# Wide projections of an attention layer: token blocks zero and one by Strassen's seven half products

## The chip, the cores and the metric

One core of a Trainium2 chip runs the whole kernel. The metric is the device time of one execution in microseconds (us). The engines are named as in the profile: PE is TensorE, DVE is VectorE, ACT is ScalarE, POOL is GpSimd, SP is SyncE; PEld is TensorE's weight load.

## The reference

One layer of a diffusion backbone: 2048 latent tokens, 256 context tokens, width 1024. One wide input projection feeds two token mixers (latent attention with a rotary key, neighbourhood attention on a 32 x 64 grid); both results are gated, projected and merged.

```python
h = rmsnorm(x, norm_g[i]) * (1 + scale) + shift
hc = rmsnorm(ctx, norm_g[i]) * (1 + scale_c) + shift_c
ckv, kr, kb, vb, cq, za, qb, zb, ga, gb = split_cols(h @ w_in[i], KV_SPLITS + Q_SPLITS)
...
oa = block_attention(qa, jnp.concatenate([ka, kca], axis=1),
                     jnp.concatenate([va, vca], axis=1), mla_scale)
ob = neighborhood_attention(heads(qb, NA_HEADS), heads(kb, NA_HEADS), heads(vb, NA_HEADS),
                            heads(c_kb, NA_HEADS), heads(c_vb, NA_HEADS), rpb[i])
ya = (oa * jax.nn.silu(za)) @ w_oa[i]
yb = (ob * jax.nn.silu(zb)) @ w_ob[i]
y = (jax.nn.sigmoid(ga) * ya + jax.nn.sigmoid(gb) * yb) @ w_out[i]
x = x + gate * y
return rmsnorm(x, final_g)
```

The change concerns `h @ w_in`: of its columns, kb, qb, za, zb (512 each) and ga, gb (1024 each) are the wide ones.

## The kernel before

**Number format.** A float32 operand is split into a high part, rounded to the matmul's reduced type by an ACT copy, and a low part, the difference, by a DVE subtraction (`split_weight`, L112 to L117). A product is then three matmuls: high by high, high by low, low by high (`mm3`, L135, which records all of them).

**Layout.** The normalised tokens lie transposed in SBUF as four blocks of 512, each with a high and a low tile of 8 x (128 x 512) (`hh`, `hl`, in pools `hT0` to `hT3`). The wide columns come in 32 chunks of 128: 0 to 3 are k, 4 to 7 q, 8 to 11 za, 12 to 15 zb, 16 to 23 ga, 24 to 31 gb. Chunks 16 and 17 are computed earlier as fillers.

**The projection stage.** One chunk is loaded (`load_chunk`, L312: `rawc`, 128 x 1024, then `whi` by ACT and `wlo` by DVE) while the one before is multiplied. `chunk` (L363 and the lines behind) runs over the token blocks in `srcs`: 24 matmuls of 128 x 512 into a PSUM bank `accm`, then an evacuation: `evac_k` (L326), `evac_q` (L341) or `evac_g` (L353 to L359, a sigmoid on ACT, for za and zb a product on DVE, and a store of 256 KB). k chunks have three blocks, since block zero is done earlier, the others four: 4 x 3 + 26 x 4 = 116 blocks.

**Raw weights.** Every raw weight of this stage goes through `raw_tile` (L306 to L309), which alternates between two pools with one raw buffer each, whatever the weight is. A load therefore waits until the weight that was loaded two calls before has been split.

**Side work.** Three generators are pumped from this loop.
- `lowrank_gen` (L599 and the lines behind): the low-rank q, k and v of the latent attention, with its stores to DRAM (`qm`, `kmS`). One step per block, for chunks below `NSIDE` = 20.
- `gate_gen` (L573): eight loads `rawg` of 512 KB with four small matmuls each. One per item from item 12.
- `presplit_gen` (L587): 16 weights of the output stage are loaded (`rawps`, 512 KB), split in two halves `ps` into the two buffers `st`, and stored (`woS`, `wfS`, L595, 512 KB each). Two per item behind item 22.

The v columns are two items of their own, `vb_load` and `vb_run` (L693, L705): each 16 tiles of 24 matmuls of 128 x 256 into `vacc`, with 256 columns of weights in pool `vw`. They stand behind items 20 and 22. The last two chunks, 30 and 31, are interleaved block by block.

**Order.** The tile framework turns the program into one order of instructions per engine and inserts the waits; most DMA loads and stores of this stage are issued by SP in program order, so an issue that waits for a buffer holds up the ones behind it. Behind the stage, SP loads `NKm` and `NQs` (L848, L849), the neighbourhood attention's keys and queries, from the stores of the k and q chunks.

The loop that sets the order:

```python
for i, (_, run_) in enumerate(items):
    cur = nxt
    if i + 1 < len(items):
        nxt = items[i + 1][0]()
    run_(cur)
    if i >= 12:
        next(gate_it, None)
    if i > NSIDE + 2:
        pump(pre_it, 2)
```

## Time and profile before

| | us |
|---|---|
| median of 3 runs | 2521.4 |
| fastest and slowest run | 2518.43, 7962.48 |
| the profiled execution, its time | 2524.23 |
| its span in the profile | 2522.5 |
| normalisation, context and fillers, about | 0 to 243 |
| projection stage | 243 to 1052 |
| attention | 1053 to 2140 |
| output stage | 2140 to 2522 |

The span runs from the first to the last instruction of the profiled execution. Busy time of an engine is the time in which it executes; a matmul's listed duration overlaps that of its neighbours, so the pace of many matmuls is read from a window or from a piece of the chain, not from one duration. The granted clock (PEclk) is given as a share of full speed.

### The profile page before, as it was taken

Reading aid. Unit: us, or ns where it says so; the run is one execution under the profiler, and the core shown is the slowest. Engines: PE = TensorE matmul, PEld = TensorE weight load, DVE = VectorE, ACT = ScalarE, POOL = GpSimd, SP = SyncE. Lnnn points to the kernel's source line nnn. Section 1 sums busy time; section 2 is a strip of 40 time slices with the busy share of each in tenths; the row PEclk is TensorE's granted clock in tenths of the full one; section 3 lists DMA queues with packets and bytes.
Section 4 is the critical chain, followed back from the end, with each engine's and each line's share of the span. In section 5 each row is a group of like instructions: output and inputs, shape, how many; then the busy total and the mean of one; then the engine's idle time right before and its main releaser. Section 6 shows DMA issues by size and latency. Waiting matters only on the chain.

```text
span 2522.5 us, 34848 instructions
## 1 busy us (share of the span) xinstructions
PE 2476.6 (98%) x12796; PEld 1841.1 (73%) x12796; DVE 1108.0 (44%) x2285; ACT 900.8 (36%) x1774; POOL 1092.7 (43%) x861
## 2 busy tenths in 40 slices
...
GB/s 270 194 92 167 260 222 193 126 163 192 194 164 92 115 214 204 179 94 43 105 33 130 39 111 39 124 36 111 39 130 36 59 173 93 256 184 164 179 146 72
DMA packets 182980, 342.86 MB, mean 136 GB/s; under 512 B 25130, under 2 KB 95950, under 8 KB 175438
## 3 DMA queue, kind: packets, MB, share of 16 engines
...
q10 hardware_dynamic: 432, 0.28, 0.0%
HBM read 214.42 MB, written 126.13 MB: 135 GB/s over the span
## 4 chain that ended last, share of the span: by engine, by line
PE 91%; DVE 3%; DMA 2%; ACT 2%; issue 1%; POOL 1%; SPq 0%; POOLq 0%; ACTq 0%; DVEq 0%
PE accm L135 26%; PE S L807 16%; PE oacc L807 10%; PE pm L807 5%; PE ya L135 5%; PE f L135 4%; PE vacc L135 4%; PE nacc L226 3%; PE no L807 3%; PE accf L135 2%; PE accx L135 1%; PE nm L807 1%; PE pstl L185 1%; PE qa_False L135 1%; ACT P L1278 1%
## 5 line engine op out<-in xcount | busy, mean ns | idle before, releaser
L1288 POOL TENSOR_TENSOR za<-za,P 128x1024 f32<-128x1024 f32 x217 | 516.4, 2380 | 97.0 <-ACT P L1278 90.3
L825 DVE TENSOR_REDUCE m<-pm 128x1 f32<-128x512 f32 (+1 forms) x640 | 385.9, 632 | 284.4 <-PE pm L807 278.0
L1278 ACT ACTIVATE P<-S 128x512 f32<-128x512 f32 x576 | 342.1, 596 | 427.9 <-PE S L807 401.3
L135 PE MATMUL accm<-hh,whi 128*128 128x512 f32 x928 | 366.7, 395 | 0.0
L135 PE MATMUL accm<-hh,wlo 128*128 128x512 f32 x928 | 366.4, 395 | 0.0
L135 PE MATMUL accm<-hl,whi 128*128 128x512 f32 x928 | 366.4, 395 | 0.0
L807 PE MATMUL oacc<-P,V 128*64 128x512 f32 x1152 | 274.9, 613 | 0.0
L807 PE MATMUL S<-qh,Kh 97*128 97x512 f32 x576 | 242.0, 420 | 9.2 <-ACT P L1278 5.1
L807 PE MATMUL S<-ql,Kh 96*128 96x512 f32 x576 | 230.4, 400 | 0.0
L807 PE MATMUL S<-qh,Kl 96*128 96x512 f32 x576 | 229.3, 398 | 0.0
L807 PE MATMUL pm<-Kh,qh 96*128 96x512 f32 (+1 forms) x640 | 214.5, 382 | 8.7 <-DVE m L825 5.8
L135 PEld LDWEIGHTS accm<-hh,whi 128*128 128x128 f32 x928 | 174.1, 188 | 42.9 <-issue 0.8
L135 PEld LDWEIGHTS accm<-hh,wlo 128*128 128x128 f32 x928 | 174.1, 188 | 42.5
L135 PEld LDWEIGHTS accm<-hl,whi 128*128 128x128 f32 x928 | 174.1, 188 | 41.5
L135 PE MATMUL ya<-u,woh 128*128 128x256 f32 x1024 | 184.9, 283 | 0.7 <-DVE t L1346 0.7
L807 PEld LDWEIGHTS oacc<-P,V 128*64 128x64 f32 x1152 | 75.7, 139 | 150.1 <-issue 150.1
L807 PEld LDWEIGHTS pm<-Kh,qh 96*128 96x128 f32 x640 | 120.2, 188 | 73.0 <-issue 29.6
L135 PE MATMUL f<-wfh,y 128*128 128x512 f32 (+1 forms) x528 | 162.2, 387 | 1.9 <-ACT y L1349 1.8
L135 PEld LDWEIGHTS ya<-u,woh 128*128 128x128 f32 x1024 | 160.1, 192 | 1.7 <-DVE t L1346 0.9
L807 PEld LDWEIGHTS S<-qh,Kh 97*128 97x128 f32 x576 | 109.5, 190 | 56.8 <-ACT P L1278 22.6
L135 PE MATMUL ya<-u,wol 128*128 128x256 f32 x512 | 144.8, 283 | 0.0
L356 ACT ACTIVATE g<-accm 128x512 f32<-128x512 f32 x88 | 52.2, 593 | 250.4 <-PE accm L135 208.1
...
## 6 DMA issues: line engine op xcount, KB each, us to landing
rawc<-in_wch SPq DMA_DIRECT2D x30, 512.0 KB
...
qR<-q SPq DMA_DIRECT2D x16, 512.0 KB
...
woS<-ps SPq DMA_DIRECT2D x16, 512.0 KB
```

The costliest lines, as they stand in the source:

```text
L135: nc.tensor.matmul(acc, a, b, start=(i == 0), stop=(i == n - 1))
L185: nc.tensor.matmul(pst[32 * j:32 * j + 32, :w], ones[:, 0:32], sq[:, :w], start=(kt < 4), stop=(kt >= 4))
L226: nc.tensor.matmul(acc[:, :n], a[:, k, sl], b[:, k, :n], start=(k == 0 and q == 0), stop=(k == KT - 1 and q == 2))
L356: nc.scalar.activation(s1, acc, AF.Sigmoid)
L807: ins = nc.tensor.matmul(*args, **kw)
L825: nc.vector.reduce_max(m5[:, qt, ci:ci + 1], pm[:, :b - a], axis=AX.X)
L1278: nc.scalar.activation(pt[:, x, :], sp, AF.Exp)
L1288: ve.tensor_tensor(za, za, pt, op=ALU.add)
```

## The change

The 26 wide chunks 4 to 15 and 18 to 31 are paired: 13 pairs of 256 columns. In a pair, token blocks zero and one against the two chunks are computed as one 2 x 2 product of halves by Strassen's scheme (in Winograd's form): the inner dimension of 1024 is halved, the two token blocks are the two columns of the token operand, and the two chunks the two columns of the weight. Seven products of 12 matmuls (L844 after) replace the 8 x 12 of four plain blocks.

- Blocks two and three of all 30 chunks are computed first, as before (`srcs = lat[2:]`), with two side steps per block. The gate and the two presplits run behind items 18 and later, chunks 20 and up.
- The v items come last: half one for tiles 8 to 15, then half zero for tiles 8 to 15 and 0 to 7. Half one for tiles 0 to 7 is loaded again at the end.
- `token_sums` builds the sums of the token halves (`t1` to `t5`), splits them and writes them into new tiles `ta`, `tb` in the pools of blocks two and three. Per k: 11 DVE, 3 POOL and 4 ACT operations of 128 x 512, for four k.
- `fast_columns` runs the pairs. Per pair it loads two raw chunks, forms the four weight sums on POOL (`s1` to `s4`), splits seven operands of 128 x 512 on ACT and DVE (`w1` to `w7`), runs the seven products into three banks `A`, `B`, `C`, of which four are accumulated on top of an earlier one, forms the sums `c1`, `u2`, `u4` on ACT and DVE, and evacuates four results.
- Then come the four k chunks of block one, and half one of v for tiles 0 to 7. The stages behind are as before.

```diff
-        srcs = lat[1:] if ci < 4 else lat
+        srcs = lat[2:]
...
+    def vb_load(hf, pl=None):
+        if pl is None and hf == 1:
             pump(side_gen, 999)
-            env["vw"] = pool(xes, "vw")
-        vw = env["vw"]
-        vhi = vw.tile([P, KT, 256], F32R, tag="vhi", name=f"vhi{hf}")
-        vlo = vw.tile([P, KT, 256], F32R, tag="vlo", name=f"vlo{hf}")
-        load_big(vw, I["wvb"][:, :, hf * 256:(hf + 1) * 256], 256, vhi, vlo, f"w{hf}")
+            env["vw"] = pool(ves, "vw")
+        vw = pl or env["vw"]
...
+    def vb_run(hf, wt, tis):
+        for ti in tis:
             vb_tile(ti, hh[ti // 4], hl[ti // 4], ti % 4, wt[0], wt[1], 2 * hf, 2)
...
-        items += [chunk_item(base + j, j, ev, 1 if base + j < NSIDE else 0) for j in range(n) if base + j not in (FILL, FILL + 1)]
-    items.insert(NSIDE, (lambda: vb_load(0), lambda wt: vb_run(0, wt)))
-    items.insert(NSIDE + 2, (lambda: vb_load(1), lambda wt: vb_run(1, wt)))
-    ev = evac_g(gbS, False)
-
-    def last_two(wt):
-        ws = (wt, load_chunk(31))
-        for sr in lat:
-            for q in range(2):
-                chunk(f"m{30 + q}", 6 + q, ws[q], [sr], ev)
-
-    items[-2:] = [(lambda: load_chunk(30), last_two)]
...
+    gate_it, pre_it = gate_gen(), presplit_gen()
...
-        if i >= 12:
+        if i >= 18:
             next(gate_it, None)
-        if i > NSIDE + 2:
             pump(pre_it, 2)
-    xes.close()
...
+    def token_sums(ph, hp, hq, pl):
+        ta, tb_ = h_tiles(2, f"ta{ph}"), h_tiles(3, f"tb{ph}")
+        def split(src, dst, k, add=None):
+            nc.scalar.activation(dst[0][:, k, :], src, AF.Copy)
+            nc.vector.tensor_tensor(dst[1][:, k, :], src, bc(dst[0][:, k, :]), op=ALU.subtract)
+        def gen():
+            for k in range(HK):
+                p1_, p2_ = [[bc(t[:, k + x * HK, :]) for t in hp] for x in range(2)]
+                q1_, q2_ = [[bc(t[:, k + x * HK, :]) for t in hq] for x in range(2)]
+                t1 = pl.tile([P, W], F32, tag="t1", name=f"t1{ph}_{k}")
+                t2 = pl.tile([P, W], F32, tag="t2", name=f"t2{ph}_{k}")
+                nc.gpsimd.tensor_tensor(t1, q1_[0], p1_[0], op=ALU.subtract)
+                nc.vector.tensor_tensor(t2, q1_[1], p1_[1], op=ALU.subtract)
+                nc.vector.tensor_tensor(t1, t1, t2, op=ALU.add)
+                split(t1, ta, k)
+                nc.vector.tensor_tensor(t2, q2_[0], t1, op=ALU.subtract)
+                nc.vector.tensor_tensor(t2, t2, q2_[1], op=ALU.add)
+                split(t2, ta, k + HK)
+                yield
+                t3 = pl.tile([P, W], F32, tag="t1", name=f"t3{ph}_{k}")
+                nc.gpsimd.tensor_tensor(t3, p2_[0], t2, op=ALU.subtract)
+                nc.vector.tensor_tensor(t3, t3, p2_[1], op=ALU.add)
+                split(t3, tb_, k + HK)
+                yield
+                t4 = pl.tile([P, W], F32, tag="t2", name=f"t4{ph}_{k}")
+                t5 = pl.tile([P, W], F32, tag="t1", name=f"t5{ph}_{k}")
+                nc.gpsimd.tensor_tensor(t4, q2_[0], q1_[0], op=ALU.subtract)
+                nc.vector.tensor_tensor(t5, q2_[1], q1_[1], op=ALU.subtract)
+                nc.vector.tensor_tensor(t4, t4, t5, op=ALU.add)
+                split(t4, tb_, k)
+                yield
+        (b11, b21), (_, b22) = halves(*hp), halves(*hq)
+        (o1, o2), (o3, o4) = halves(*ta), halves(*tb_)
+        return gen(), [b11, o2, o3, o1, b21, o4, b22]
+    pairs = []
+    for base, n, dst, silu in ((4, 4, None, 1), (8, 4, zaS, True), (12, 4, zbS, True),
+                               (16, 8, gaS, False), (24, 8, gbS, False)):
+        ev = evac_g(dst, silu) if dst is not None else evac_q
+        js = [j for j in range(n) if base + j not in (FILL, FILL + 1)]
+        pairs += [(base, js[i], js[i + 1], ev) for i in range(0, len(js), 2)]
+    def load_pair(ph, i):
+        base, a, b, _ = pairs[i]
+        return [raw_tile(I["wch"][base + j].rearrange("p k m -> p (k m)"), f"s{ph}_{base + j}").rearrange("p (x f) -> p x f", x=2)
+                for j in (a, b)]
+    def fast_columns(ph, p, q, bops, raws):
+        with ExitStack() as es:
+            wop = pool(es, "wop", 3)
+            wt_ = pool(es, "wt")
+            ct = pool(es, "ct")
+            slots = [0]
+            def slot(nm):
+                i = slots[0] % 7
+                slots[0] += 1
+                if i < 4:
+                    return env["cw"][i // 2].tile([P, KT, P], F32R, tag=("whi", "wlo")[i % 2], name=nm)
+                return wop.tile([P, KT, P], F32R, tag="op", name=nm)
+            def operand(src, nm):
+                t = slot(nm)
+                f = t.rearrange("p k m -> p (k m)")
+                nc.scalar.activation(f[:, :W], src, AF.Copy)
+                nc.vector.tensor_tensor(f[:, W:], src, bc(f[:, :W]), op=ALU.subtract)
+                return [(t[:, k, :], t[:, HK + k, :]) for k in range(HK)]
+            def tmp(tag, nm):
+                return wt_.tile([P, W], F32, tag=tag, name=nm)
+            def prep(i, ra, rb):
+                nm = f"{ph}_{i}"
+                a11, a12, a21, a22 = ra[:, 0], ra[:, 1], rb[:, 0], rb[:, 1]
+                yield operand(a11, f"w1{nm}")
+                s1, s2 = tmp("s1", f"s1{nm}"), tmp("s2", f"s2{nm}")
+                nc.gpsimd.tensor_tensor(s1, a21, a22, op=ALU.add)
+                nc.gpsimd.tensor_tensor(s2, s1, a11, op=ALU.subtract)
+                yield operand(s2, f"w6{nm}")
+                s3 = tmp("s3", f"s3{nm}")
+                nc.gpsimd.tensor_tensor(s3, a11, a21, op=ALU.subtract)
+                yield operand(s3, f"w7{nm}")
+                yield operand(s1, f"w5{nm}")
+                yield operand(a12, f"w2{nm}")
+                yield operand(a22, f"w4{nm}")
+                s4 = tmp("s3", f"s4{nm}")
+                nc.gpsimd.tensor_tensor(s4, a12, s2, op=ALU.subtract)
+                yield operand(s4, f"w3{nm}")
+            def product(acc, w_, x_, first):
+                n = 0
+                for (ah, al), (bh, bl) in zip(w_, x_):
+                    for a, b in ((ah, bh), (ah, bl), (al, bh)):
+                        nc.tensor.matmul(acc, a, b, start=(first and n == 0), stop=(n == 3 * HK - 1), skip_group_check=True)
+                        n += 1
+            def bank(nm):
+                return psA.tile([P, 512], F32, tag="acc", name=nm)
+            g = prep(0, *raws)
+            ops = list(g)
+            for i, (base, ja, jb, ev) in enumerate(pairs):
+                nm = f"{ph}_{i}"
+                nops = []
+                g = iter(())
+                if i + 1 < len(pairs):
+                    g = prep(i + 1, *load_pair(ph, i + 1))
+                def run(m, acc, first):
+                    product(acc, ops[m], bops[m], first)
+                    o = next(g, None)
+                    if o is not None:
+                        nops.append(o)
+                A = bank(f"A{nm}")
+                run(0, A, True)
+                c1 = ct.tile([P, W], F32, tag="c1", name=f"c1{nm}", bufs=2)
+                nc.scalar.activation(c1, A, AF.Copy)
+                B = bank(f"B{nm}")
+                run(1, B, True)
+                u2 = ct.tile([P, W], F32, tag="u2", name=f"u2{nm}")
+                nc.vector.tensor_tensor(u2, B, c1, op=ALU.add)
+                C_ = bank(f"C{nm}")
+                run(2, C_, True)
+                run(3, B, False)
+                u4 = ct.tile([P, W], F32, tag="u4", name=f"u4{nm}")
+                nc.vector.tensor_tensor(u4, B, c1, op=ALU.add)
+                nc.vector.tensor_tensor(u4, C_, u4, op=ALU.add)
+                ev(jb, q, u4, W)
+                run(4, A, False)
+                ev(ja, p, A, W)
+                run(5, C_, False)
+                nc.vector.tensor_tensor(u2, C_, u2, op=ALU.add)
+                ev(jb, p, u2, W)
+                run(6, B, False)
+                nc.vector.tensor_tensor(c1, B, c1, op=ALU.add)
+                ev(ja, q, c1, W)
+                ops = nops
+    tg, bops = token_sums(0, (hh[0], hl[0]), (hh[1], hl[1]), tl)
+    raws = load_pair(0, 0)
+    pump(tg, 99)
+    ves.close()
+    fast_columns(0, 0, 1, bops, raws)
+    hes2.close()
+    with ExitStack() as es:
+        vw2 = pool(es, "vw2", side="right")
+        wt2 = vb_load(1, vw2)
+        nxt = load_chunk(0)
+        for j in range(4):
+            cur = nxt
+            if j < 3:
+                nxt = load_chunk(j + 1)
+            chunk(f"n{j}", j, cur, lat[1:2], evac_k)
+        vb_run(1, wt2, range(8))
+    tes.close()
     hes.close()
     p1.close()
```

How the instructions stand now. First ACT, before, around `whi27`, the split of chunk 27: `g1_2` and `g1_3` are the evacuations of the last two blocks of chunk 25, `ps` the halves of the presplit weights.

```order
L116 ACTIVATE ps6_0_7606<-rawps6_7604 128x512
L116 ACTIVATE ps6_1_7610<-rawps6_7604 128x512
L356 ACTIVATE g1_2_7435<-accm25_2_7410 128x512
L116 ACTIVATE whi27_7488<-rawc27_7486 128x1024
L356 ACTIVATE g1_3_7463<-accm25_3_7438 128x512
L116 ACTIVATE ps7_0_7616<-rawps7_7614 128x512
L356 ACTIVATE g2_0_7517<-accm26_0_7492 128x512
L116 ACTIVATE ps7_1_7620<-rawps7_7614 128x512
L356 ACTIVATE g2_1_7545<-accm26_1_7520 128x512
```

In the changed kernel the same place on ACT reads:

```order
L356 ACTIVATE g2_3_5326<-accm26_3_5301 128x512
L116 ACTIVATE whi27_5269<-rawc27_5267 128x1024
L356 ACTIVATE g3_2_5386<-accm27_2_5361 128x512
L116 ACTIVATE ps12_0_5337<-rawps12_5335 128x512
L116 ACTIVATE ps12_1_5341<-rawps12_5335 128x512
L356 ACTIVATE g3_3_5414<-accm27_3_5389 128x512
L116 ACTIVATE ps13_0_5347<-rawps13_5345 128x512
L116 ACTIVATE ps13_1_5351<-rawps13_5345 128x512
L116 ACTIVATE whi28_5357<-rawc28_5355 128x1024
L116 ACTIVATE ps14_0_5425<-rawps14_5423 128x512
```

Before, `whi27` stood in the middle of chunk 25's evacuations, two chunks ahead of its use. Now it stands behind the last evacuation of chunk 26 (`g2_3`), and `whi28` behind that of chunk 27 (`g3_3`) and all four `ps` of its item. SP, in the changed kernel, from the gate load of item 24 on:

```order
L309 DMA rawg6_5329<-in_wmod 128x1024
L309 DMA rawps12_5335<-in_wout 128x1024
L309 DMA rawps13_5345<-in_wout 128x1024
L359 DMA gbS3_151<-g3_2_5386 128x512
L598 DMA wfS_158<-ps12_0_5337 128x2x512
L598 DMA wfS_158<-ps12_1_5341 128x2x512
L309 DMA rawc28_5355<-in_wch 128x1024
L359 DMA gbS3_151<-g3_3_5414 128x512
L598 DMA wfS_158<-ps13_0_5347 128x2x512
L598 DMA wfS_158<-ps13_1_5351 128x2x512
L309 DMA rawg7_5417<-in_wmod 128x1024
L309 DMA rawps14_5423<-in_wout 128x1024
```

The load `rawc28` stands behind the two stores of `ps12`, which is loaded in the same item, and behind the first store of chunk 27 (`g3_2`); before, it stood between two stores of chunk 25. DVE, in the changed kernel, from the place where block two's tiles come free, at the start of the products:

```order
L753 TENSOR_TENSOR hlta0_6424<-t10_0_6431,hhta0_6423 128x512
L753 TENSOR_TENSOR hlta0_6424<-t20_0_6432,hhta0_6423 128x512
L771 TENSOR_TENSOR t30_0_6442<-t30_0_6442,hl0_193 128x512
L753 TENSOR_TENSOR hltb0_6426<-t30_0_6442,hhtb0_6425 128x512
L777 TENSOR_TENSOR t50_0_6448<-hl1_787 128x512
L778 TENSOR_TENSOR t40_0_6447<-t40_0_6447,t50_0_6448 128x512
L753 TENSOR_TENSOR hltb0_6426<-t40_0_6447,hhtb0_6425 128x512
L762 TENSOR_TENSOR t20_1_6455<-hl1_787,hl0_193 128x512
L763 TENSOR_TENSOR t10_1_6454<-t10_1_6454,t20_1_6455 128x512
L765 TENSOR_TENSOR t20_1_6455<-hh1_786,t10_1_6454 128x512
L753 TENSOR_TENSOR hlta0_6424<-t10_1_6454,hhta0_6423 128x512
```

Here `hlta0` and `hltb0` are the low parts of `ta` and `tb`; these rows are one k and the start of the next, and none of them stands in the kernel before.

## Rows read from the trace of the kernel before

**Rows 1.** The page, engines' busy time and the chain that ended last by engine.

```profile
PE 2476.6 (98%) x12796; PEld 1841.1 (73%) x12796; DVE 1108.0 (44%) x2285; ACT 900.8 (36%) x1774; POOL 1092.7 (43%) x861
...
PE 91%; DVE 3%; DMA 2%; ACT 2%; issue 1%; POOL 1%; SPq 0%; POOLq 0%; ACTq 0%; DVEq 0%
```

**Rows 2.** Chain in order of time, projections: start us, us, what.

```profile
503.26 11.20 PE accm L135 x48
...
732.73 45.43 PE vacc L135 x384
```

**Rows 3.** Windows: us, busy (x) of PE, PEld, DVE, ACT, POOL; PEclk, DMA share, GB/s.

```profile
243.00:505.00 262.00, 262.00 (x1131) 210.98 (x1131) 56.30 (x76) 79.93 (x134) 40.39 (x60) 1.00 0.63 202
...
690.00:870.00 180.00, 180.00 (x1164) 161.25 (x1163) 27.76 (x42) 34.85 (x70) 14.56 (x26) 1.00 0.41 127
```

**Rows 4.** The page, DMA issues.

```profile
rawc<-in_wch SPq DMA_DIRECT2D x30, 512.0 KB
...
woS<-ps SPq DMA_DIRECT2D x16, 512.0 KB
```

**Rows 5.** Windows with full DMA engines, columns as before.

```profile
10.00:20.00 10.00, 7.39 (x55) 2.99 (x54) 3.23 (x13) 7.12 (x12) 0.06 (x1) 1.00 1.00 395
...
270.00:280.00 10.00, 10.00 (x45) 8.04 (x44) 1.71 (x3) 4.68 (x9) 1.27 (x2) 1.00 0.97 345
```

**Rows 6.** Timeline, 940 to 957 us: start, us, engine, what [idle before <-releaser].

```profile
941.84 0.33 SPq L309 DMA_DIRECT2D rawps<-in_wout  x1
...
945.68 0.63 ACT L116 ACTIVATE ps<-rawps 128x512 fp32r<-128x512 f32 x1 [4.65 <-DMA rawps<-in_wout]
...
947.25 1.20 SPq L595 DMA_DIRECT2D wfS<-ps  x2
948.54 0.71 SPq L309 DMA_DIRECT2D rawps<-in_wout  x1
...
953.69 1.15 ACT L116 ACTIVATE ps<-rawps 128x512 fp32r<-128x512 f32 x2 [2.12 <-DMA rawps<-in_wout]
```

**Rows 7.** Timeline, 880 to 889 us.

```profile
881.85 0.72 SPq L309 DMA_DIRECT2D rawps<-in_wo  x1
...
887.76 1.15 ACT L116 ACTIVATE ps<-rawps 128x512 fp32r<-128x512 f32 x2 [3.39 <-DMA rawps<-in_wo]
```

**Rows 8.** Groups by line, 240 to 1052 us: busy, mean ns | idle before, releaser.

```profile
L117 DVE TENSOR_TENSOR wlo<-rawc,whi 128x1024 fp32r<-128x1024 f32 x30 | 36.8, 1225 | 165.2 <-ACT whi L116 165.2
...
L116 ACT ACTIVATE whi<-rawc 128x1024 fp32r<-128x1024 f32 x29 | 30.7, 1058 | 106.4 <-PE accm L135 104.5 <-DMA rawc<-in_wch 1.9
...
L117 DVE TENSOR_TENSOR ps<-rawps,ps 128x512 fp32r<-128x512 f32 x32 | 21.5, 691 | 103.1 <-ACT ps L116 103.0
```

**Rows 9.** Chain in order of time, end of the projections.

```profile
1051.77 0.60 ACT g L356
...
1060.53 0.28 PE nm L807 x2
```

**Rows 10.** Groups by line of POOL, whole span.

```profile
L1184 POOL TENSOR_TENSOR za<-za 128x512 f32<-128x512 f32 x31 | 39.7, 1279 | 1.6
...
L622 POOL DMA_DIRECT2D qm<-sqr x64 | 31.8, 505 | 71.3 <-DVE sqr L618 69.2 <-issue 2.1
```

**Rows 11.** Timeline, 2113 to 2123 us, POOL and DVE.

```profile
2113.04 4.88 POOL L1288 TENSOR_TENSOR za<-za,P 128x1024 f32<-128x1024 f32 x2 [2.78 <-ACT P L1278]
...
2115.62 2.57 DVE L1105 TENSOR_TENSOR z<-z,rz 128x256 f32<-128x256 f32 x1
...
2122.53 0.42 DVE L1105 TENSOR_TENSOR z<-z,rz 128x256 f32<-128x256 f32 x1 [0.30 <-DMA rz<-rmS]
```

**Rows 12.** Timeline, 299 to 306 us.

```profile
299.57 0.37 SPq L339 DMA_DIRECT2D kB<-kb  x1
...
304.86 1.15 ACT L337 ACTIVATE kb<-k 128x512 fp32r<-128x512 f32 x2 [1.08 <-DMA kB<-kb]
```

**Rows 13.** Timeline of SP's queue, 1030 to 1045 us.

```profile
1035.97 0.50 SPq L848 DMA_DIRECT2D NKm<-kR  x1
```

30 lines of the change are left out of this document (20 added, 10 removed).

## Prediction

> **What bounds the kernel now.** Read first the busy shares and the chain of work that ended last: TensorE is busy for 98% of the span, and the chain runs over TensorE for 91% [rows 1]. So a microsecond of matmul removed is worth a microsecond, as long as TensorE stays fed. Then the same chain in order of time, in the projection stage: 48 `accm` matmuls are one piece of 11.20 us, 384 `vacc` matmuls one of 45.43 [rows 2]. A 128x512 matmul therefore costs 11.20/48 = 0.2333 us of the chain (its listed duration of 395 ns overlaps its neighbours), a 128x256 one of the v tiles 0.118. Last the windows of that stage: TensorE is never idle in the two shown, while DVE and ACT are at 15 to 31% and the DMA engines at 41 to 63% with 127 to 202 GB/s [rows 3]. The other engines have room on average; what has to be read is whether they have it where the change puts the work.
>
> **Part 1, the products: a gain of 36.4 us.** Before, the wide chunks take 116 blocks of 24 matmuls, 2784. After, blocks two and three of 30 chunks take 60 x 24 = 1440, 13 pairs take 7 products of 12 matmuls, 1092, and the k chunks of block one 4 x 24 = 96: 2628. 156 fewer x 0.2333 = 36.4 us. The shape is the same, so the price is the row's. The v tiles stay 768 matmuls.
>
> **Part 2, the plain half: 36 us lost at chunks 22 to 29.** A chunk now has two blocks, 11.2 us, or 11.7 with the gate's four small matmuls, where it had 22.4. But the pump stayed per item: one gate load and two weight splits behind each. Per item that is 512 KB of `rawc`, 512 of `rawg`, 2 x 512 of `rawps`, 4 x 512 of stores of `ps` (`woS` or `wfS`) [rows 4] and 2 x 256 of `g`: 4608 KB or 4.72 MB in 11.7 us, 403 GB/s. Windows in which the DMA engines are full carry 345 GB/s when loads and stores mix, 395 when nearly all are large loads [rows 5]. At 345 the item takes 13.7 us, 2.0 too long.
> The order of loads is worse than the rate. All raw loads alternate between two buffers, and with c, g, ps, ps, c the chunk always lands in the buffer of the first ps of its item. So `rawc28` waits until `rawps12` has landed and been split, and `rawps12` until `wlo27` is done: two loads in series per item, as SyncE's new order shows. A 512 KB load is ready 3.84 us after its issue (941.84 to 945.68), 5.15 behind two stores (948.54 to 953.69) [rows 6], and 5.9 in a busier place (881.85 to 887.76) [rows 7]. Durations: `whi` 1.06, `wlo` 1.23, a half split 0.63 on ACT [rows 6] and 0.69 on DVE [rows 8], `g` 0.60 [rows 9]; two store issues 1.2 [rows 6].
> An odd item, from the start of `whi27`: `wlo27` ends at 2.3, block two at 8.0, its `g` at 8.8 (ACT's new order has it ahead of ps12), the two halves at 10.1, DVE's at 10.8, stores issued, `rawc28` issued at 11.5, ready at 15.3 to 16.7. An even item: `rawps14` issued at 2.4, ready at 6.2 to 7.5, split by 8.2 to 9.5, `rawc29` issued at 9.4 to 10.7, ready at 13.6 (where `g` of block three ends) to 15.9. Mean 14.5 to 16.3, less 11.7: 2.8 to 4.6 us idle per item. Seven such items (chunks 23 to 29), at 3.7, make 26. Before them chunk 22: ACT does ps0 only after the `g` of the last block of chunk 21, so TensorE waits for 0.2 + 0.6 + 1.25 + 0.7 + 1.2 + a load of 3.84 to 5.15 + 1.06 = 8.8 to 10.2; I take 9.5. Together 36. The bottom is the rate alone, 8 x 2.0 = 16; the top has all loads at 5.9: odd and even then take 17.4, 7 x 5.7 + 11 = 51. Before, the same chain had 22.4 us to run in, and [rows 6] show ACT, not TensorE, waiting for it.
>
> **Part 3, the start of the products: 12 us.** The token sums are 44 DVE operations with both inputs in SBUF, 12 on GpSimd and 16 ACT copies. Their results go into the buffers of blocks two and three, so the second operand half can be written only when v tile 15 is done; eight tiles of 2.84 = 22.7 us are left, and 2.8 of the first product: 25.5. In DVE's order 35 operations stand from there to the operand of the second product: 35 x 0.69 = 24.1 [rows 8], which just fits. Ten GpSimd operations of 1.28 us [rows 10] run beside them. Where GpSimd adds, a DVE operation with two SBUF inputs ends only when GpSimd's does: at 2115.62 a `z` of 0.42 us takes 2.57 [rows 11]. Added rather than overlapped: 24.1 + 10 x 1.28 = 36.9, 11.4 late, with the first waits 12. Bounds: 1 (all overlapped) to 16 (each ACT copy waited for as well).
> The Trainium skill states the rule behind that row in "SBUF — State Buffer", section "Who interferes with whom": a DVE instruction with two SBUF inputs contends with a GpSimd instruction that reads SBUF, and whoever comes first holds the port for its whole length. The trace agrees (2.57 for 0.42); without the rule this part would cost 1 and the forecast would be 11 us lower.
>
> **Part 4, the small ones: 13 us.** The last v item has one buffer for its weights, so it splits only after the item before it is done: 0.63 + 0.69 and then two 256 KB pieces that wait for their buffers, partly beside 36 matmuls: 2.5 us (1 to 4).
> The side work goes twice as fast, two steps per block. In the k blocks ACT waits for the previous `kB` store, 5.3 us from issue (299.57 to 304.86) [rows 12]; with its two copies of 0.63 that is a period of about 7.0 against a block of 5.6 + 2 x 0.7 = 7.0, and at the rope steps GpSimd needs 8 x 0.505 = 4.0 us per step [rows 10] against TensorE's 4.2. Both just fit on durations that were measured at half the load: 5 us (0 to 20).
> In a pair TensorE needs 84 x 0.2333 = 19.6 us; DVE 16 x 0.69 = 11.0, ACT 12 x 0.61 = 7.3, GpSimd 4 x 1.28 = 5.1. The latest deadline: product six waits for two sums after product four, with an operand split between them on DVE, 3 x 0.69 + 0.2 = 2.3 us beside the 2.8 of product five. 0.5 to spare, except where a GpSimd operation or q's two stores get in between: 4 us over 13 pairs (0 to 20).
> The tail: the load of `NKm`, once issued 16 us before the last `accm` was done [rows 9, 13], now stands in SyncE's order behind the store of the last v tile, so it is issued some 2 us after it. Its first user, `nm`, came 9 us after the last `accm` [rows 9]: 2 us (0 to 5).
> DMA for 30 more raw chunks and half of wvb (16 MB) falls into stretches with 107 GB/s (a pair: 2 x 512 + 4 x 256 KB in 19.6 us) and costs nothing there.
>
> **The sum.** -36.4 + 36 + 12 + 2.5 + 5 + 4 + 2 = +25 us. The rows come from an execution of 2524.2 us (span 2522.5); the median of the runs is 2521.4, 2.8 lower. So 2521.4 + 25 = 2546. Lows: -36.4 + 16 + 1 + 1 = -18. Highs: -36.4 + 51 + 16 + 4 + 20 + 20 + 5 = +80.
>
> **Rivals.**
> A. The gain comes through. If the loads run ahead of the splits, the window costs little (16 by rate, or less where ps work slips past item 29), and the sums overlap: -36.4 + 10 + 5 = -21, 2500. For it: DMA at 60% and ACT mostly idle there before. Against it: SyncE's and ACT's order fixes two loads in series, and 403 GB/s was seen in no mixed window. 0.14.
> B. The pairs are bound by the vector chain, not TensorE. If GpSimd's sums land late (a raw chunk 2 us late is enough), they hold DVE off the split before the second sum, and each pair loses 1.3 to 2.5 us: 13 x 2 = 26 in place of 4, so +47, 2568. It decides once the deadline of 2.8 us is missed. Against it: on time, GpSimd's four operations end before product four does. 0.12.
> C. The side work chokes the first half. In the k and q blocks 2.05 MB per 7.0 us are 293 GB/s, 85% of the 345 of a full window; if stores then take 7 us in place of 5.3, 16 blocks lose 1 to 1.5 us each and the rope steps 5: +20 more, 2566. 0.12.
> The forecast itself: 0.55, own range 2526 to 2566. Left over 0.07.
>
> **How the numbers follow.** The time is the forecast's, 2546. The range of 2510 to 2583 cuts off the best part of A and the case that B and C come together. 2% (50 us) is about what a measurement of this kernel can tell from no change. Faster by more is out of reach of 36.4 us: 0.01. Slower by more needs over 2572: half of B and C (0.12), the forecast's upper tail (0.04): 0.16. Within: 0.83.
>
> **What would show it.** Right: the plain chunks 22 to 29 come every 14.5 to 16.5 us instead of 11.7, with TensorE waiting for `whi` or `wlo`, and behind them a DMA of `rawc`; DMA at over 0.85 there. A gap of some 12 us spread over the first pair, with DVE's sums at more than 0.69 us beside GpSimd. Pairs every 19.6 to 20 us. Wrong: chunks 22 to 29 every 11.7 us (A), pairs of 21.5 us or more (B), k and q blocks of more than 7.5 us (C).

## The result and the profile after

The changed kernel takes 2598.5 us (median; 2592.06 to 2602.22) where the kernel before takes 2519.9 beside it: a ratio of 1.031 (95% interval 1.029 to 1.033), 79 us slower. One execution of the kernel before took 7962.48 us; nothing here explains it, and the ratio leaves it out. The forecast was 2546 with a range up to 2583, and the time lies above that range: it was wrong. The profiled execution took 2602.0 us with a span of 2600.2, 77.7 above the span before. The working below is in times of these two spans.

The page of the kernel after, engines' busy time and granted clock in 40 slices, answers to [rows 1]:

```profile
PE 2473.2 (95%) x12640; PEld 1825.1 (70%) x12640; DVE 1266.2 (49%) x2493; ACT 981.1 (38%) x1902; POOL 1181.6 (45%) x925
...
PEclk9999999988998999999999999999999999999999
```

156 matmuls are gone, as forecast, yet TensorE is busy for nearly as long as before (2473.2 us against 2476.6) and its share falls from 98 to 95%. The slices with an 8 are in the projections, and they are the first sign of something that the forecast left out: a lower clock. The same windows as [rows 3] show it by stage (columns as there: busy time and matmuls of PE, then PEld, DVE, ACT, POOL; clock, DMA share, GB/s). Windows of the kernel after:

```profile
269.00:375.00 106.00, 95.81 (x380) 74.44 (x379) 25.99 (x33) 39.08 (x65) 27.16 (x39) 0.94 0.86 259
375.00:539.00 164.00, 162.12 (x708) 129.89 (x706) 60.63 (x83) 52.52 (x84) 53.69 (x96) 1.00 0.76 233
539.00:568.00 29.00, 11.46 (x48) 8.95 (x48) 6.11 (x9) 9.23 (x16) 10.36 (x21) 0.74 0.66 199
568.00:696.00 128.00, 105.18 (x415) 74.43 (x416) 29.16 (x37) 33.52 (x53) 0.61 (x1) 0.88 0.81 275
696.00:794.00 98.00, 97.17 (x698) 90.84 (x698) 25.72 (x32) 21.50 (x45) 9.88 (x7) 1.00 0.19 61
794.00:831.00 37.00, 24.43 (x88) 18.46 (x87) 30.50 (x34) 13.28 (x25) 18.52 (x12) 0.77 0.19 66
831.00:875.00 44.00, 40.95 (x169) 32.15 (x168) 23.98 (x34) 18.54 (x32) 10.16 (x8) 0.96 0.55 194
875.00:1072.00 197.00, 197.00 (x846) 157.83 (x845) 94.77 (x133) 72.32 (x119) 51.42 (x39) 1.00 0.37 115
1072.00:1140.00 68.00, 61.11 (x349) 51.63 (x349) 25.91 (x45) 20.14 (x35) 10.92 (x7) 0.95 0.80 205
...
553.00:574.00 21.00, 5.58 (x13) 3.94 (x14) 4.50 (x6) 4.47 (x7) 3.98 (x8) 0.51 0.66 212
574.00:604.00 30.00, 23.24 (x101) 16.63 (x99) 6.58 (x9) 8.03 (x14) 0.00 (x0) 0.94 0.80 270
604.00:611.00 7.00, 5.94 (x16) 3.81 (x20) 1.23 (x1) 0.96 (x1) 0.00 (x0) 0.53 0.86 286
...
799.00:816.00 17.00, 8.03 (x18) 5.87 (x19) 16.80 (x18) 6.30 (x12) 9.77 (x6) 0.50 0.14 47
```

How to read them: window less PE busy is TensorE's idle time, 75.8 us over the first nine rows (before, the projections had 0.2, and 3.4 in the 70 us behind them). And where TensorE had stood idle, the granted clock falls to 0.50, the lower of its two levels, 1.2 GHz: 16 matmuls in the 7 us from 604, where the full clock (2.4 GHz) does 30. Only the pairs from 875 on run as the forecast has them: 197.00 of 197 us busy, clock 1.00. Between 269 and 1140, 56 us of matmuls run at the lower clock. The price of one is in the timeline of the kernel after, around the first plain chunk with presplit, 545 to 574 us (columns as in [rows 6]; the SP, ACT and PE rows):

```profile
547.80 8.30 SPq L359 DMA_DIRECT2D gaS<-g  x4
...
551.58 1.08 ACT L356 ACTIVATE g<-accm 128x512 f32<-128x512 f32 x2 [3.74 <-DMA gaS<-g]
555.15 0.60 ACT L356 ACTIVATE g<-accm 128x512 f32<-128x512 f32 x1 [2.48 <-DMA gaS<-g]
...
556.16 0.62 ACT L116 ACTIVATE ps<-rawps 128x512 fp32r<-128x512 f32 x1
...
557.62 5.53 SPq L598 DMA_DIRECT2D woS<-ps  x2
561.40 0.63 ACT L116 ACTIVATE ps<-rawps 128x512 fp32r<-128x512 f32 x1 [4.62 <-DMA woS<-ps]
...
563.20 0.47 SPq L309 DMA_DIRECT2D rawc<-in_wch  x1
...
567.27 1.06 ACT L116 ACTIVATE whi<-rawc 128x1024 fp32r<-128x1024 f32 x1 [0.82 <-DMA rawc<-in_wch]
...
568.38 0.79 PE L135 MATMUL accm<-hh,whi 128*128 128x512 f32 x1 [17.59 <-ACT whi L116]
...
571.09 0.63 PE L135 MATMUL accm<-hh,wlo 128*128 128x512 f32 x1
571.51 0.63 PE L135 MATMUL accm<-hh,whi 128*128 128x512 f32 x1
571.94 0.63 PE L135 MATMUL accm<-hl,whi 128*128 128x512 f32 x1
...
573.89 0.39 PE L135 MATMUL accm<-hh,whi 128*128 128x512 f32 x1
574.12 0.40 PE L135 MATMUL accm<-hl,whi 128*128 128x512 f32 x1
```

Start to start a 128x512 matmul takes 0.427 us at the lower clock (571.09, 571.51, 571.94) and 0.233 from 573.89 on. So 56 us at the lower clock hold 56 x (1 - 0.233/0.427) = 25 us of loss. The same rows show chunk 22: SyncE needs 8.30 us for four stores of `g`, whose sigmoid on ACT waits 3.74 and 2.48 us for earlier stores of `g` to land, then 5.53 for two stores of a split weight, whose split waits 4.62 for the store before it; `rawc22` is issued only at 563.20, and TensorE waits 17.59 us.

Waits of PE in the kernel after, 240 to 1150 us (total, times, longest):

```profile
PE accm L135 <- ACT whi L116: 38.7, 8, 17.6
PE B L844 <- ACT w L815: 9.9, 1, 9.9
PE nm L971 <- issue: 6.5, 1, 6.5
PE B L844 <- DVE u L877: 4.7, 2, 3.1
PE ka L135 <- DVE sk L621: 4.0, 1, 4.0
```

The stages, with the losses by pace. Starts are those of every 24th `accm` and every 84th product matmul in the trace. Blocks 4 to 15 count against 7.0 us, the pace at which they run undisturbed in e7 below, the blocks behind them against their undisturbed pace in e7 or c3b; the eight plain chunks against 94.8, their time in e10; a pair against 19.6. The last column is what the matmuls at the lower clock cost, at 0.454 of their time.

| stretch | forecast (bounds) | loss | idle in it | clock in it |
|---|---|---|---|---|
| products | -36.4 | -36.4 | | |
| before the projections (start 247.2, was 242.8) | 0 | 4.4 | | |
| side work, blocks 4 to 15 (269.6 to 375.0, for 84) and the 23 behind (3.4) | 5 (0 to 20) | 25 | 12.4 | 5.7 |
| chunk 22 (23.4 for a block of 5.6) | 9.5 | 17.8 | 17.6 | 0 |
| chunks 22 to 29 (568.4 to 701.9: 133.5 for 94.8) | 26 | 38.7 | 22.4 | 12.3 |
| v items | 2.5 | 1.6 | 0.8 | 0 |
| first pair (36.5) | 12 (1 to 16) | 16.9 | 12.6 | 3.6 |
| other pairs (24.5 for the third, then 19.6) | 4 (0 to 20) | 5.0 | 3.1 | 1.4 |
| tail, first `accn` to the end (1529.4, for 1520.2) | 2 (0 to 5) | 9.2 | 6.9 | 2.2 |
| sum | +25 | +82 | 75.8 | 25 |

The 1520.2 of the tail are 1470.7 of the kernel before, 45.1 of k and v work moved there, and 4.4 for 20 `pm` matmuls of the attention, which before ran inside its projections (858.7 to 870.4 us). The sum is 4 above the 77.7 measured; of the losses themselves some 18 show neither as idle time nor as low clock.

Two rows differ from execution to execution. The projections start at 240.9 to 248.4 us in the 20 traces kept: at 242.8 and 245.4 in two executions of one kernel (c3b), at 242.8 or less in the five traces without a stretch of low clock in the first 45 us, at 245.1 or more in all others. And the stretch from the first `accn` to the end takes 1521.9 to 1531.8 us in the nine runs whose program is the same there: a loss of 2 to 12 in place of the 9.2.

### The profile page after: what moved, and what is told of

The parts are those of the page before. It is cut to its first block, busy times and chain, and to the rows that moved or that the text cites. A ratio compares the mean times of both kernels' runs of the same rounds, so it can differ in the third digit from the quotient of the medians.

```text
span 2600.2 us, 35100 instructions
## 1 busy us (share of the span) xinstructions
PE 2473.2 (95%) x12640; PEld 1825.1 (70%) x12640; DVE 1266.2 (49%) x2493; ACT 981.1 (38%) x1902; POOL 1181.6 (45%) x925
## 4 chain that ended last, share of the span: by engine, by line
PE 50%; DMA 3%; DVE 2%; ACT 1%; POOL 1%; issue 1%; SPq 1%; POOLq 0%; ACTq 0%; DVEq 0%
PE S L971 15%; PE oacc L971 10%; PE pm L971 5%; PE ya L135 5%; PE f L135 5%; PE no L971 3%; PE nm L971 1%; PE vacc L135 1%; DMA rz<-rzS 1%; ACT P L1442 1%; PE nc L971 1%; DMA Kh<-kmS 1%; PE zp L971 0%; POOL o L1270 0%; DMA g<-gbS 0%
## 5 line engine op out<-in xcount | busy, mean ns | idle before, releaser
L135 PE MATMUL accm<-hh,whi 128*128 128x512 f32 x480 | 196.9, 410 | 40.1 <-ACT whi L116 38.7
L135 PE MATMUL accm<-hh,wlo 128*128 128x512 f32 x480 | 195.3, 408 | 0.4
L135 PE MATMUL accm<-hl,whi 128*128 128x512 f32 x480 | 195.3, 407 | 0.0
L135 PEld LDWEIGHTS accm<-hh,whi 128*128 128x128 f32 x480 | 93.4, 194 | 67.5 <-ACT whi L116 42.2
L971 PEld LDWEIGHTS S<-qh,Kl 96*128 96x128 f32 x576 | 110.5, 192 | 25.8
L971 PEld LDWEIGHTS S<-ql,Kh 96*128 96x128 f32 x576 | 110.6, 192 | 10.4
L135 PEld LDWEIGHTS f<-wfh,y 128*128 128x128 f32 x528 | 97.9, 188 | 24.6 <-DMA wfh<-wfS 2.8
```

The source lines that it names most:

```text
L135: nc.tensor.matmul(acc, a, b, start=(i == 0), stop=(i == n - 1))
L971: ins = nc.tensor.matmul(*args, **kw)
```

## The experiments

A time without an interval is of one execution; the changed kernel's own four span 10 us, so such times are read together with the stretch of the trace that the edit touches. Every kernel but the last ones is the changed one with the edit shown.

**The window of the plain chunks.** Theory: the shared raw buffers and SyncE's order put the loads in series. Rival: the rate of the DMA engines.

e1: the presplit weights load into half buffers of their own, at the same places in the program.

```diff
-            raw = raw_tile(src, f"ps{q}")
...
+                raw = tl.tile([P, W], F32, tag=f"t{n + 1}", name=f"rawp{q}_{n}")
+                nc.sync.dma_start(raw, src[:, ns])
```

> Edit: in the plain half the presplit weights come through two half buffers of their own (256 KB each), no longer through the two raw buffers that the wide chunks use; the amount loaded and stored is the same. In the changed kernel chunks 23 to 28 came every 17.1 us instead of 11.7, and chunk 22 waited 17.6 us. Theory S (two loads in series, because the raw buffers are shared): chunks 23 to 28 come every 11.7 to 12.5 us, the wait before chunk 22 goes, and the time falls by 35 to 55 us to about 2545 to 2565. Rival R (the rate of the DMA engines: 4.72 MB per item at 345 GB/s): they come every 13.7 to 14.5 us, DMA share over 0.9, time about 2570 to 2580. Rival B (the two buffers of ps: a half is split only when the store of the half before last has landed, some 5 us, four halves per item): every 13 us or more at a DMA share that is not full, time about 2570 to 2580. If the pitch stays at 17, none of the three.

2567.65 us, 31 less. Windows of e1:

```profile
544.00:661.00 117.00, 107.12 (x450) 81.42 (x451) 26.30 (x33) 34.25 (x53) 10.58 (x22) 0.94 0.79 256
...
596.20:613.90 17.70, 17.70 (x85) 13.74 (x82) 5.38 (x7) 5.86 (x10) 0.00 (x0) 1.00 0.93 310
613.90:660.60 46.70, 39.40 (x161) 29.04 (x160) 11.94 (x15) 14.29 (x22) 0.61 (x1) 0.93 0.92 305
```

450 matmuls in 117 us, where after does 463 in 157 (539 to 696), with the DMA engines at the same 0.79. Some 12 us of the stretch's 56 stay. The rate alone was not the limit: e1 moves 310 GB/s from 596 to 614 us without an idle microsecond of TensorE, and c3b below 302, where after moves 275 and loses. But the edit moved the work too. In the changed kernel the first of the 32 weight halves is split at 556.2, ahead of chunk 22, and all of them are stored by the end of chunk 29; in e1 the first split comes at 585.0, behind two of the chunks, 21 weight halves are stored by the end of chunk 29 (666.2), and the others beside the last chunks and the v items, up to 707.9. How much of the 45 us went with the shared buffers, and how much with the 11 halves that no longer lie there, is not told apart.

e8: the same, and three halves per item in place of four, over more items.

```diff
-            pump(pre_it, 2)
+            pump(pre_it, 3)
```

> Edit: presplit through its own half buffers, as in the run with own buffers, but three halves per item over eleven items instead of four over eight. That run still lost 12 us between chunks 24 and 28. If the rate is what was left (4.72 MB per item at four halves, 3.93 at three, 336 GB/s in 11.7 us), the loss of the stage falls under 5 us and the time to about 2560; if it was the store of ps (two buffers), a half every 3.9 us is still more than 5 us per two buffers allow only in bursts: 2560 as well. If 12 us stay, the cause is another, such as the order on SyncE.

2571.37 us, and the same 12 us are lost as in e1, at chunks 26 to 29. It is no test of a smaller amount: 20 halves are stored in the window, in e1 21, and the last at 709.2. In both, ACT, in order, waits for `rawp` loads ahead of `whi` (24.6 us in 11 waits from 600 to 665 us in e1).

e2: the same loads, three halves per pair instead of in the window.

```diff
-            pump(pre_it, 2)
...
+            pump(pre_it, 3)
```

> Edit: the presplit leaves the plain half altogether and runs in the pairs, three halves per pair, through half buffers of its own; the gate loads stay, one per item. All three theories of the plain half (loads in series, rate, buffers of ps) expect chunks 22 to 29 every 11.7 us with TensorE at full clock, which takes 54 us out of that stretch: about 2545 if the pairs stay at 19.6 us. What is told apart is the price in the pairs: three more splits of 0.69 us on DVE make 13.1 us of 19.6, so by busy time nothing; by the deadline of product six (0.5 us to spare by my sum) each pair loses 0.7 to 2 us, 2555 to 2570.

2560.6 us. The plain chunks come every 11.8 us at full clock; pairs two to eight take 21.0 to 27.2, the ninth and tenth, with the last six halves, 19.8 and 19.6, as do those without presplit. The work is not free there: part of its wait moves from `whi` to the sums of the pairs (B, C and A wait 17.4 us for DVE's `u` and ACT's `c`).

e10: the presplit's loads, splits and stores on GpSimd, in the plain half, through half buffers of its own, three halves per item over twelve items; the gate loads start two items later.

```diff
-                nc.sync.dma_start(bc(dst[:, :, ns].rearrange("a p f -> p a f")), bc(s1))
+                split_weight(raw, s1[:, 0, :], s1[:, 1, :], True)
+                nc.gpsimd.dma_start(bc(dst[:, :, ns].rearrange("a p f -> p a f")), bc(s1))
```

> Edit: the presplit stays in the plain half, but its loads, splits and stores all go over GpSimd (which is idle from 570 to 760 us), with half buffers of its own, three halves per item; the gate loads start two items later. In the run with own buffers 12 us were still lost there, with ACT in order before the wide chunk's split waiting for the presplit's load. Theory (what is left is the order on ACT and SyncE): chunks 22 to 29 come every 11.7 us, time about 2552 to 2558. Rival (the rate of the DMA engines): 10 us stay lost, about 2565.

2586.38 us. Windows of e10, then its waits (DVE, 640 to 745):

```profile
556.00:651.00 95.00, 95.00 (x439) 72.93 (x442) 11.50 (x9) 18.21 (x27) 51.98 (x68) 1.00 0.78 252
680.00:745.00 65.00, 36.68 (x264) 35.78 (x263) 7.33 (x10) 7.69 (x18) 37.04 (x46) 0.74 0.50 169
```

```profile
DVE t L764 <- POOL ps L117: 29.7, 1, 29.7
DVE vlo L117 <- ACT vhi L116: 23.6, 1, 23.6
```

The window is perfect: eight chunks without an idle microsecond, with the DMA engines at 0.78. But 15 of the 32 weight halves are stored in it, the others up to 730.8, and the first of the token sums, which shares the half buffers, waits 29.7 us in DVE's order for GpSimd's last subtraction; behind it stands the `vlo` that the v item needs. So the engine and the smaller amount are not told apart here. c3b below does both as well, with 18 of them in the chunks; e1 has 21 in a stretch 10 us longer, and both reach 0.92 of the DMA engines. c3b loses nothing there, so what was left in e1 was not the rate, but the buffers (c3b has three `st` and three raw halves) or the order on ACT and SyncE. The wait ahead of chunk 22 is gone in e1, e10 and c3b alike, and in all three the first weight half is stored only behind the start of that chunk (at 586.5, 570.8 and 551.0).

The Trainium skill ("DMA: Bandwidth & Descriptors", section "Issuing engines are not separate DMA queues") says that issuing DMAs on another engine saves only the small time of starting them. By the rows of chunk 22 more was at stake, SyncE's 8.30 and 5.53 us of waits between its issues; no run here moves the issuing alone.

**The side work of the first half.** Theory (rival C of the prediction): k's steps at double rate overrun ACT's stores.

e3: one step per block for the first chunks.

```diff
-        items += [chunk_item(base + j, j, ev, 2) for j in range(n) ...
+        items += [chunk_item(base + j, j, ev, 1 if base < 8 else 2) for j in range(n) ...
```

> Edit: one step of side work per block instead of two in the k and q chunks (the first 16 blocks), two behind. In the changed kernel the stretch of blocks 4 to 15 lost 16.5 us (idle 10.2 and 12.7 at half clock). Theory C (side stores and k stores share two buffers, and the doubled pace does not let them land): that loss falls under 3 us, and since the side work then runs 8 blocks longer, into the chunks where the presplit is, up to 5 us come back there: about 2582 to 2590. Rival (the loads of the first raw weights are late, whatever the side work): the loss stays over 10 us, and the time over 2590.

2617.2 us. Blocks 6 to 14 run at 6.3 us, their pace with one step, and the stretch's loss shrinks to about 8, all in blocks 4 and 5. But the side work then meets presplit: two blocks take 36.7 and 34.6 us. Waits of PE in e3, 540 to 760:

```profile
PE accm L135 <- ACT whi L116: 60.7, 7, 25.9
```

e7: k and q chunks alternate with za and zb, at two steps.

```diff
+    items[:16] = [items[k // 2 + 8 * (k % 2)] for k in range(16)]
```

> Edit: the first 16 chunks alternate between k or q and za or zb; nothing else. A k block stores 768 KB and a q block 768 KB, a za block 256 KB, so the side work's stores meet half the rate of others. Theory (the first half loses time because stores of k and q and of the doubled side work do not land in time): the loss of blocks 4 to 15 falls from 16.5 us to under 6, time about 2587. Rival (the first steps of the side work wait for their own chain of loads, splits and stores): the wait of blocks 4 to 6 stays at 10 us or more.

2600.18 us. Blocks 5 to 20 run at 7.0 us or faster, all but one; block 4 takes 17.0, 4.1 of it waiting for the load `cnk`. What the k blocks gain is lost at blocks 31, 32 and 37 (13.8, 10.4 and 11.7 us), where TensorE waits for a sigmoid (5.8) and for the loads `cnq` (4.3): zero in sum.

e11: za and zb ahead of k and q.

```diff
+    items[:16] = items[8:16] + items[:8]
```

> Edit: the 16 first chunks in another order, za and zb before k and q; nothing else. The doubled side work's first steps, which store the most, then lie beside blocks that store 256 KB instead of 768. Theory (stores that do not land in time): blocks 4 to 15 lose under 5 us instead of 16.5, time about 2587, if the k and q blocks find room later. Rival (the start of the side work is a chain of its own): 10 us stay at blocks 4 to 6.

2616.76 us: block 4 takes 19.6 us, blocks 5 to 20 are perfect, then k and q stall beside the rope steps (10.9, 16.1, 13.1 us). e12: a third `st` buffer, and the buffers of the token sums reserved only after the side work.

```diff
-        env["st"] = pool(es, "st", 2)
+        env["st"] = pool(es, "st", 3)
...
-    tl = pool(tes, "tl")
...
+            pump(side_gen, 999)
+            tl = pool(tes, "tl")
```

> Edit: a third buffer st (k, q, sk, sqr and ps all go through st), and the buffers of the token sums are reserved only after the side work, which makes the room for it. Theory (in blocks 4 to 15 and before chunk 22 TensorE waits because st has two buffers and each store takes some 5 us to land): blocks 4 to 15 lose under 8 us instead of 16.5, chunk 22's wait falls from 17.6 to under 10; time about 2578 to 2585. Rival (the DMA engines are full there, over 0.9 from 280 to 320 us): a buffer more changes nothing, 16 us stay lost in blocks 4 to 15.

2609.66 us. Blocks 4 to 15 lose 14.7 in place of 21.4, and chunk 22 still waits (22.1): a third buffer takes a third of the first and nothing of the second. The tail lost more here, 31 us of it at the lower clock from 1117. The projections start at 240.9 in place of 247.2, but that is no work of the edit: c2 below starts at 241.3 without it, c3 at 246.6 with it.

What is left is the rival that was named with e12, full DMA engines. Windows of the kernel after:

```profile
280.00:320.00 40.00, 36.00 (x143) 28.51 (x142) 9.08 (x12) 15.85 (x27) 11.06 (x16) 0.91 0.93 280
```

0.93 of the DMA engines speak for it; e7 and e11, which put chunks with less to store there, don't tell it from waits in series. And the first block of side work, block 4, takes 11.2 us or more in every run of this document: that start was never cured.

**The start of the products.** e9: all token sums on DVE.

```diff
-                nc.gpsimd.tensor_tensor(t1, q1_[0], p1_[0], op=ALU.subtract)
+                nc.vector.tensor_tensor(t1, q1_[0], p1_[0], op=ALU.subtract)
```

> Edit: the 12 GpSimd operations of the token sums go to DVE; nothing else. In the changed kernel product one waits 10 us for the sums and the first and third pair together lose 22 us, with DVE operations beside GpSimd at 0.8 to 1.7 us instead of 0.69. Theory (GpSimd's adds hold the DVE operations beside them up for their whole length, so the two add): without them the chain is 46 operations of 0.69 = 32 us in place of 35 to 40, every one at 0.69, and the first pair falls by 3 to 6 us; time about 2594. Rival (they do overlap, and the chain is set by the waits between ACT, DVE and GpSimd): 12 more operations of 0.69 on DVE make it 4 to 8 us longer, time about 2604.

2592.21 us; the first pair takes 33.2 in place of 36.5. Groups of DVE in the first pair, 794 to 831 us, of the kernel after (columns as in [rows 8]):

```profile
L816 DVE TENSOR_TENSOR w<-s,w 128x512 fp32r<-128x512 f32 x7 | 8.3, 1206 | 3.3 <-ACT w L815 3.2
...
L762 DVE TENSOR_TENSOR t<-hl,hl 128x512 f32<-128x512 f32 x1 | 1.6, 1633 | 0.0
```

and waits of PE in e9, 785 to 880:

```profile
PE B L844 <- DVE u L877: 8.0, 2, 4.8
PE B L844 <- ACT w L815: 3.7, 1, 3.7
```

DVE's 0.69 us becomes 1.2 to 1.6 beside GpSimd, as Part 3 had it. With three sums of each group taken off GpSimd the wait for `w` falls from 9.9 to 3.7 us, but that for `u` rises from 4.7 to 8.0: GpSimd's weight sums stay beside DVE, which has more to do. The contention is real, and what the edit frees of it is 3 of the 17 us.

e4: two of the four k chunks ahead of the pairs, as work to wait behind.

```diff
+    k_chunks(0, 2)
...
+        k_chunks(2, 4)
```

> Edit: two of the four k chunks of block one run ahead of the pairs, between the last v tile and the first product, instead of behind the pairs. 11.2 us more TensorE work then lies beside the token sums. In the changed kernel the first pair took 36.5 us instead of 19.6. Theory: the sums are a chain of some 40 us that starts when block two is free; the first pair falls to 22 to 27 us and the time to about 2585 to 2590, the tail unchanged. Rival: the first pair waits for its own operands (weight sums on GpSimd), so that it stays at 33 us or more wherever it starts, and the time stays within 4 us of 2598.

2596.05 us: first pair 22.7, but 11.4 us of wait ahead of it; the operand is late by DVE's order, and 11 us of cover in front only move the wait. e6: the same, and the first pair's operands ahead of the rest of the token sums in the program.

```diff
-            g = prep(0, *raws)
-            ops = list(g)
+            ops = list(prep(0, *raws))
+            pump(tg, 99)
```

> Edit: as the run with two k chunks ahead of the pairs, and the first pair's weight operands come before the token sums: the buffers of the weight sums lie apart from the v weights, and w1, w6 and w7 go to buffers that no k chunk uses. In the run before, the first pair fell from 36.5 to 22.7 us, but TensorE waited 11.4 us for its first operand, which DVE made behind all the sums. Theory (the sums take 36 to 40 us from block two's release, the rest was order): the wait before the first product falls under 2 us, first pair 20 to 24 us, time about 2583. Rival (DVE is simply full from block two's release on: 36 sums and 7 operands at 0.9 us): the wait only moves between operands and sums, sum of both still 12 us or more, time 2592 to 2598.

2600.78 us: no wait ahead of the first product, first pairs 28.3 and 21.6 (10.7 lost in place of 21.9). The time doesn't show it: the tail loses some 6 us more (1.7 of it for v's last weights, which two k chunks cover in place of four), and blocks 4 to 38 some 4, without a change of their own.

**The tail.** e5: the last v tiles in the order 4 to 7, 0 to 3, their stores issued by GpSimd in place of SyncE.

```diff
-        vb_run(1, wt2, range(8))
+        env["q"] = nc.gpsimd
+        vb_run(1, wt2, [4, 5, 6, 7, 0, 1, 2, 3])
+        env["q"] = nc.sync
```

> Edit: the last v item runs tiles 4 to 7 before tiles 0 to 3, and stores them over GpSimd's queue. NKm lies where block one's tiles lay, so in the changed kernel its load had to wait for tile 7 and for the v stores in front of it on SyncE, and TensorE then idled 6.5 us at the start of the attention and ran 4.6 us at half clock (8.8 lost). Theory (NKm's load is late, by place and by queue): block one is now free 11.4 us earlier, NKm's load starts some 9 us earlier relative to the last v tile, the idle time goes, time about 2589. Rival (the attention waits for Kh, whose load took 15.3 us): idle time of over 4 us stays, now behind Kh, time over 2594.

2592.86 us; from the first `accn` to the end 1518.2 in place of 1529.4. Timeline of the kernel after, end of the projections (answers to [rows 9, 13]):

```profile
1122.01 1.08 SPq L393 DMA_DIRECT2D vS<-v  x2
1123.14 2.14 SPq L1317 DMA_DIRECT2D NQs<-cS  x1
1125.33 0.52 SPq L1012 DMA_DIRECT2D NKm<-kR  x1
...
1135.40 0.85 PE L971 MATMUL nm<-NKm,NQs 112*128 112x264 f32 x2 [6.50 <-issue]
```

In e5 the same `NKm` is issued at 1115.79, 10 us ahead of the last v matmul, and `nm` doesn't wait. So the 6.5 us were a load behind the last stores in SyncE's order; the new queue and the new order of the tiles are not told apart. The 11 us hold more than that: 5 of them lie over 125 us behind the first `accn`, in code that the edit doesn't touch, and the same code varies by 10 us from run to run.

**Together.** c2: e10, e11, e9, e6 and e5 in one kernel.

> Edit: together the presplit over GpSimd, za and zb first, the token sums on DVE, two k chunks ahead of the pairs with the first pair's operands before the sums, and the last v tiles of block one first over GpSimd's queue. If the losses are separate, they add: 54 us of the plain half to some 3, 16.5 of the first blocks to 5, 22 of the first pairs to 8, 11 at the start of the attention to 5: 2598 less 83 = 2515. If one is handed on to the next stage, over 2530.

2567.66 us; e10's stall at the v items and e11's stalls stay. c3: three `st` buffers, e7's order, presplit on GpSimd with the buffers of the products (so that no token sum waits for it), e9, e6, and both v halves whole, without a second load.

```diff
+    for hf in range(2):
+        items.append((lambda hf=hf: vb_load(hf), lambda wt, hf=hf: vb_run(hf, wt, list(range(8, 16)) + list(range(8)))))
```

> Edit, together: three buffers st; k, q and za, zb chunks alternate; the presplit over GpSimd with buffers that are not those of the token sums, so that DVE no longer waits for GpSimd before the v items (34 us in the run before); sums on DVE; the v halves one after the other, so that nothing is reloaded; two k chunks ahead of the pairs and two behind, no v tiles behind. Expected if the losses are separate: first half 15 us lost, plain chunks 2, first pairs 8, start of the attention 8 (its loads have 11 us of cover instead of 34): 2520 less 36 plus 33 = 2517. If the uncovered loads at the end cost over 15 us, over 2525.

2546.47 us. The first half loses 8 us, the window nothing; first pairs 22.9 to 23.6. But at the start of the attention TensorE waits 18.4 us for the load of `Kh`, with 34 us at the lower clock: nothing stands behind the k chunks to cover its loads. c3b: c3, with the last v tiles behind the k chunks again, as in e5.

```diff
+        wt2 = vb_load(1, vw2)
...
+        vb_run(1, wt2, [4, 5, 6, 7, 0, 1, 2, 3])
```

> Edit: as the run before it, but the v order and the tail of the run with everything together: half one of v is loaded again and its tiles 4 to 7 and 0 to 3 come last. Against the run before it this tells what the end of the stage costs: there 34 us of TensorE work cover the attention's loads, but the v weights have 11 us of cover for their own load. Expected: start of the attention 5 to 12 us lost, time 2515 to 2522.

2516.11 us. c4 moves the reloaded v weights off the place of `bn`, a load of the attention, and the v stores to ACT's queue; c4k has three k chunks ahead as well.

```diff
+        env["q"] = nc.scalar
...
+        pool(es, "pad", side="right").tile([P, 4096], F32, name="pad")
...
-    k_chunks(0, 2)
+    k_chunks(0, 3)
```

> Edit, on the run before with v last: the place of the reloaded v weights is moved down by 16 KB, so that they no longer lie where bn of the attention goes, and the v stores are issued by ACT itself instead of SyncE or GpSimd. In the run before, bn could be loaded only after the last v tile (13 us, and TensorE at half clock for 17 us behind it: 9 lost), and the switch between the v halves lost 6.6 us behind v stores on SyncE. Theory: both go, 2516 less 10 to 15, so 2501 to 2506, clear of the kernel before by 15 to 20 us. Rival (the loads at the start of the attention are bound by rate or by Kh): 5 us or less come back, 2511 or more.

> Edit: as the run beside it, with three k chunks ahead of the pairs and one behind. In the run before, DVE was still behind with the sums in the first pair (9.9 us lost, 3.8 more in the next two). 5.6 us more cover in front take about 5 us off there; behind the pairs the v weights' load (some 9 us with the splits) then has 5.6 us of cover instead of 11.2, and costs up to 5 us and the clock. Expected: within 5 us of the run beside it; faster by 3 to 5 if the load at the end stays hidden.

Ratios to before 1.0052 (1.0034 to 1.0071) and 1.0090 (1.0073 to 1.0108): worse than c3b. SyncE, ahead of `Kh`'s load, now waits for v stores to land (6.5 us the longest); the load is issued 1.7 us behind the start of the last v matmul, in c3b 9.7 ahead of it, and TensorE waits 9.5 us for it in c4, 10.6 in c4k. The first pair of c4k (32.2, in c4 28.8) wins nothing from a third chunk. c3b again, timed:

> The run with v last, unchanged, now timed in rounds against the kernel before. In its one look it took 2516.1 us against 2521.2 of the kernel before on the same chip. If the scheme's 36.4 us come through less the 37 us that were still lost there, less what the kernel before loses itself, the ratio is 0.997 to 1.000, so no difference at 2% and a gain of 0 to 8 us; over 1.002 would mean that the one look was a lucky one.

2522.22 us against 2523.64, ratio 0.9995 (0.9981 to 1.0009): no difference. Windows of it:

```profile
243.00:539.00 296.00, 292.69 (x1264) 235.15 (x1263) 101.28 (x135) 105.74 (x171) 89.45 (x151) 1.00 0.80 254
539.00:653.00 114.00, 114.00 (x543) 88.27 (x542) 13.30 (x10) 21.50 (x31) 76.09 (x98) 1.00 0.83 278
...
580.00:610.00 30.00, 30.00 (x139) 23.10 (x139) 3.85 (x3) 4.89 (x7) 22.89 (x28) 1.00 0.92 302
...
745.00:830.00 85.00, 78.79 (x319) 62.27 (x318) 44.62 (x64) 33.49 (x57) 21.47 (x16) 0.95 0.45 154
830.00:1030.00 200.00, 199.58 (x923) 163.41 (x922) 82.22 (x117) 69.66 (x116) 51.51 (x46) 1.00 0.42 129
1030.00:1100.00 70.00, 62.84 (x267) 40.77 (x265) 43.27 (x96) 19.76 (x33) 35.17 (x22) 0.88 0.75 154
```

The first half runs with 3.3 us idle, the window with none, at 0.83 of the DMA engines and 0.92 in the middle of it. 15 us are still lost at the first pairs, some 10 behind the last chunk (17.1 us at the lower clock from 1040), 8 at blocks 4 and 6, a few at the start and at the v items: about what the products save. The same seven products in another order are thus some 75 us faster than the changed kernel, and level with the plain ones. No version found beats before.

## Why the prediction was wrong

The sign was right, and the places: each stretch named in Parts 2 to 4 lost time. What made +78 of +25:

- **The step that failed: the sum charged each wait its idle time and nothing else.** The losses forecast were 61.5 us, the idle time measured 75.8. The clock came on top: 56 us of matmuls at 0.427 in place of 0.233, 25 us, in no part and no bound of the prediction. That this is a price of the waits is read from the rows, where the low stretches stand at and behind TensorE's gaps, and from e10 and c3b, where a window without gaps keeps the clock at 1.00. "DVE and ACT are at 15 to 31%" and "TensorE is never idle" described a kernel that had no gaps to pay for.
- **Part 2 (36; 57 lost).** For chunks 22 to 29 the idle time was near: 22.4 us against 26, with a load behind it as forecast; up to the last they come every 17.4 us in place of the 14.5 to 16.5 of the forecast. The clock adds 12. That the two loads in series made it is consistent with e1 and not isolated by it. Chunk 22 was mis-sized: 9.5 forecast, 17.6 idle. I counted ACT's `g` ahead of the first split, but not that SyncE needs 8.30 us for the stores of that `g`, nor the wait of the split halves for the store buffer (4.62). Rival A's premise, room on the DMA engines and on ACT, held in c3b, in another order and with fewer halves under the chunks.
- **Part 4, side work (5; 25 lost) and tail (2; 9.2).** "Both just fit on durations that were measured at half the load" was the weak sentence: with the DMA engines at 0.86 ACT waits up to 5.5 us for a store of `sk`, and behind it TensorE for `sk`. Rival C had late stores at 25 and a chance of 0.12; that the size agrees is luck, since it put the loss into 16 even blocks and the rope steps, while 14.5 of the 21.4 in blocks 4 to 15 lie in blocks 4 to 6, where the side work starts. About 7 of the 25 show neither as idle nor as low clock. For the tail I priced one late issue, of `NKm`, at 2; behind it in SyncE's order stand ten more loads of the next stage, all late by the same wait.
- **Part 3 (12; first pair 16.9).** Idle 12.6: right. The remainder is clock. Contention of DVE and GpSimd was there at the size of [rows 11], but e9 shows only 3 us of it on the path; the order of DVE's work (e4, e6) decides more. So the number was right partly by luck.
- **Not seen:** 4.4 us ahead of the projections, which vary between executions of one kernel.
- **Right:** the products, 19.6 us for every pair from the fourth on, so rival B fell; v items under 2.5.

The highs of the sum's own parts came to +80 and held the result; the stated range, cut at +62, treated it as unlikely that several parts come out high together. They did, and every gap cost clock as well, which those highs did not hold: that +80 covers +78 is no credit to them.
